# A row-gradient kernel: two transfer queues with gated loads become one queue that takes three loads and three stores in turn

## The chip, the cores and the metric

The kernel runs on one core of a Trainium2 chip. The core has a vector engine (DVE in the profile), a scalar engine (ACT), a GpSimd engine (POOL), a sync engine (SP) that computes nothing and only issues transfers, and a matrix engine that this kernel leaves idle. Sixteen DMA engines move data between the device's memory (HBM) and the on-chip buffer (SBUF, 128 partitions). An engine that issues a transfer puts it on its own queue: the profile names SP's queue q1 and ACT's queue q10. The metric is the time of one execution on the device, in microseconds; lower is better.

## The reference

```python
def setup_inputs():
    return {
        "x": np.random.randn(8192, 8192).astype(np.float32),
    }

def reference(x: np.ndarray) -> np.ndarray:
    return np.gradient(x, axis=1)
```

Along each row of 8192 numbers, an inner result is half the difference of its right and left neighbour, `(x[j+1] - x[j-1]) / 2`. The first result is `x[1] - x[0]` and the last is `x[8191] - x[8190]`, without the half. The input has 268.44 MB and so has the output; nothing is reused between rows.

## The kernel before

A tile is 256 rows: each of the 128 partitions holds `R = 2` consecutive rows, 16384 floats or 64 KB in one contiguous run, 8.39 MB in all. There are `nsets = 32` tiles and `NB = 3` buffers, the slots; tile i lives in slot i % 3. A slot is 64 floats longer than a tile: the input lies at offset `SH = 64` and the result is written over it at offset 0, so one slot serves for the load, the arithmetic and the store of its tile.

Each tile goes through five steps.

- `load` (line 69) brings the tile in. It is issued by SP, on q1.
- `put_aside` (line 78), on POOL, computes the four end differences of each partition (two rows, left and right) from the input and keeps them in `ends`. It waits for the load.
- `halve` (line 90), on DVE, is one custom instruction that subtracts and halves over the whole tile, 16382 numbers in each partition. It waits for `put_aside`, because it overwrites the input.
- `place` (line 104) copies the four kept ends over the wrong values that `halve` left at the row ends. It runs on ACT for odd tiles and on DVE for even ones.
- `store` (line 108) sends the tile out. It is issued by ACT, on q10, for the tiles 0 to 30.

The order of work is written out by hand inside a critical section with semaphores of its own (lines 44 to 54). The first three loads are issued at once. Each later load is gated by two waits of SP:

```python
                nc.sync.wait_ge(ld[(i - 1) % NB], 16 * ld_n[(i - 1) % NB])
                nc.sync.wait_ge(st[k], 16 * st_n[k])
```

The first of these (line 67) holds load i back until load i - 1 has landed, so that after the first three never more than one load is under way. The second (line 68) waits until the store of tile i - 3 has left the slot. The DMA engines thus find loads on q1 and stores on q10 and serve both queues at the same time.

The last tile is treated apart: it is halved, placed (on ACT) and stored in four pieces of half a row, 16 KB in each partition, and these four stores are issued by SP on q1. At the end SP waits for every store (lines 134 to 137).

Of the kernel before, what the change touches and what calls it, by code (L numbers as in the profile page):

```python
# [1 line left out]

# [4 lines left out]


@with_exitstack
def kernel(  # L10
    ctx: ExitStack,
    tc: tile.TileContext,
    x: bass.AP,
    out: bass.AP,
):

    nc = tc.nc
    P = nc.NUM_PARTITIONS
    n, m = x.shape
    R = 2
    NB = 3  # L30
    SH = 64
    W = R * m
    PIECES = 2 * R
    nsets = n // (P * R)
    f32 = x.dtype

    x_sets = x.rearrange("(s p t) m -> s p (t m)", p=P, t=R)
    out_sets = out.rearrange("(s p t) m -> s p (t m)", p=P, t=R)

    pool = ctx.enter_context(tc.tile_pool(name="pool", bufs=1))  # L40
    slots = [pool.tile([P, SH + W], f32, name=f"slot{k}", tag=f"slot{k}") for k in range(NB)]
    ends = pool.tile([P, nsets, R, 2], f32, name="ends", tag="ends")

    with tc.tile_critical():  # L44
        ld = [nc.alloc_semaphore(f"ld{k}") for k in range(NB)]
        st = [nc.alloc_semaphore(f"st{k}") for k in range(NB)]
        st_last = [nc.alloc_semaphore(f"st_last{q}") for q in range(PIECES)]

        aside = [nc.alloc_semaphore("aside"), 0]
        halved = [nc.alloc_semaphore("halved"), 0]  # L50
        placed = {
            nc.vector: [nc.alloc_semaphore("placed_dve"), 0],
            nc.scalar: [nc.alloc_semaphore("placed_act"), 0],
        }

        def done(ins, counter):
            ins.then_inc(counter[0])
            counter[1] += 1
            return counter[0], counter[1]

        ld_n, st_n = [0] * NB, [0] * NB

        def load(i):
            k = i % NB
            if i >= NB:

                nc.sync.wait_ge(ld[(i - 1) % NB], 16 * ld_n[(i - 1) % NB])
                nc.sync.wait_ge(st[k], 16 * st_n[k])  # L68
            nc.sync.dma_start(out=slots[k][:, SH : SH + W], in_=x_sets[i]).then_inc(ld[k], 16)
            ld_n[k] += 1  # L70

        def put_aside(i):

            k = i % NB
            xin = slots[k][:, SH : SH + W].rearrange("p (t m) -> p t m", m=m)
            nc.gpsimd.wait_ge(ld[k], 16 * ld_n[k])
            return done(
                nc.gpsimd.tensor_sub(  # L78
                    out=ends[:, i, :, :],
                    in0=xin[:, :, 1 : m : m - 2],  # L80
                    in1=xin[:, :, 0 : m - 1 : m - 2],
                ),
                aside,
            )

        def halve(b, c0, c1, ready):

            nc.vector.wait_ge(*ready)
            return done(
                nc.vector._custom_dve(  # L90
                    dve_ops.TENSOR_TENSOR_REDUCE_SUB_MAX,
                    out=b[:, c0:c1],
                    in0=b[:, SH + c0 + 1 : SH + c1 + 1],
                    in1=b[:, SH + c0 - 1 : SH + c1 - 1],
                    s0=0.0,
                    s1=0.5,
                ),
                halved,
            )

        def place(engine, out, in_, ready):
            engine.wait_ge(*ready)
            copy = nc.scalar.copy if engine is nc.scalar else nc.vector.tensor_copy
            return done(copy(out=out, in_=in_), placed[engine])  # L104

        def store(engine, i, c0, c1, ready, sem):
            engine.wait_ge(*ready)
            engine.dma_start(out=out_sets[i, :, c0:c1], in_=slots[i % NB][:, c0:c1]).then_inc(sem, 16)

        for i in range(NB):  # L110
            load(i)
        for i in range(nsets):
            k = i % NB
            b = slots[k]
            at = put_aside(i)
            if i < nsets - 1:
                at = halve(b, 1, W - 1, at)
                rows = b[:, 0:W].rearrange("p (t m) -> p t m", m=m)
                at = place(nc.scalar if i % 2 else nc.vector, rows[:, :, 0 : m : m - 1], ends[:, i, :, :], at)
                store(nc.scalar, i, 0, W, at, st[k])  # L120
                st_n[k] += 1
            else:

                step = W // PIECES
                for q in range(PIECES):
                    c0, c1 = q * step, (q + 1) * step
                    row, right = divmod(q, 2)
                    at = halve(b, c0 + 1 - right, c1 - right, at)
                    edge = c1 - 1 if right else c0
                    put = place(nc.scalar, b[:, edge : edge + 1], ends[:, i, row, right : right + 1], at)  # L130
                    store(nc.sync, i, c0, c1, put, st_last[q])
            if i + NB < nsets:
                load(i + NB)
        for k in range(NB):
            nc.sync.wait_ge(st[k], 16 * st_n[k])
        for q in range(PIECES):
            nc.sync.wait_ge(st_last[q], 16)


# [1 line left out]
_INS = ['x']  # L141
_OUTS = [((8192, 8192), 'float32')]


# [23 lines left out]
```

## Time and profile before

| what | value |
|---|---|
| median of four executions | 1251.9 us (1250.61 to 1252.5) |
| the profiled execution | 1250.61 us |
| its span in the profile | 1248.5 us |
| moved | 268.44 MB read, 268.44 MB written, mean 430 GB/s |
| DVE busy | 554.4 us, 44% of the span |
| `halve` of a whole tile, x31 | 17224 ns each |
| `halve` of a quarter tile, x4 | 4424 ns each |
| `put_aside`, x32 | 199 ns each |
| `place` on ACT (four ends), x15 / on DVE, x16 | 198 ns / 172 ns each |
| transfers: loads / stores of a tile / stores of a quarter | 32 / 31 / 4 |

The profile lists the instructions of one execution with their times. The span runs from the first to the last thing the core did; about 2 us of the execution's time lie around it. Besides instructions the trace has a record of each packet that a DMA engine moved: its queue, start, duration and size. A tile transfer consists of 128 packets of 64 KB, eight on each of the 16 DMA engines, and one record of 4 bytes per DMA engine that counts up the semaphore. The engine's name is not in a packet's record, but on each DMA engine the next packet starts 4 ns before the recorded end of the one before, so the records can be strung into 16 sequences.

### The profile page before, as it was taken

How to read it: one execution, taken by the hardware profiler on the slowest of the kernel's cores; microseconds unless marked ns; L12 is line 12 of the kernel's file. 1: busy time of each engine (PE TensorE's matmuls, PEld its weight loads, DVE VectorE, ACT ScalarE, POOL GpSimd, SP SyncE). 2: the span in 40 equal slices, each digit the busy share in tenths (PEclk: the TensorE clock that was granted, in tenths of full speed). 3: DMA queues.
4: the chain of work that ended last, by engine and by line, in shares of the span. 5: the costliest groups of instructions: out<-in, count | busy, mean ns of one | idle time of the engine just before them, and what ended most of it. 6: DMA issues, size and time to landing. Idle time of an engine off the chain costs nothing.

```text
span 1248.5 us, 259 instructions
## 1 busy us (share of the span) xinstructions
DVE 554.4 (44%) x51; ACT 5.0 (0%) x20; POOL 6.6 (1%) x36
## 2 busy tenths in 40 slices
DVE  2841452445533455334553345543355433554235
ACT  0000000000000000000000000000000000000000
POOL 0000000000000000000000000000000000000000
DMA  9999999999999999999999999999999999999998
GB/s 403 437 437 437 426 435 420 428 430 437 437 435 435 428 435 424 428 435 437 433 428 430 435 433 428 437 437 435 437 426 430 437 435 422 437 420 437 437 437 370
DMA packets 9649, 536.88 MB, mean 430 GB/s; under 512 B 1072, under 2 KB 1072, under 8 KB 1072
## 3 DMA queue, kind: packets, MB, share of 16 engines
q1 hardware_dynamic: 5184, 276.83, 51.7%
q10 hardware_dynamic: 4464, 260.05, 48.1%
q14 instruction: 1, 0.01, 0.0%
HBM read 268.44 MB, written 268.44 MB: 430 GB/s over the span
## 4 chain that ended last, share of the span: by engine, by line
DMA 96%; DVE 3%; issue 0%; POOL 0%; ACT 0%; SPq 0%
DMA slot<-in_x_dram 93%; DMA out_dram<-slot 3%; DVE slot L90 3%; POOL ends L78 0%; ACT slot L104 0%; DVE slot L104 0%; SPq L163 0%; SPq L68 0%; SPq L44 0%
## 5 line engine op out<-in xcount | busy, mean ns | idle before, releaser
L90 DVE CUSTOM_DVE_ANT_0 slot<-slot 128x16382 f32<-128x16382 f32 (+1 forms) x35 | 551.6, 15761 | 680.7 <-POOL ends L78 680.6
L78 POOL TENSOR_TENSOR ends<-slot 128x4 f32<-128x4 f32 x32 | 6.4, 199 | 1211.0 <-DMA slot<-in_x_dram 1211.0
L104 ACT COPY slot<-ends 128x4 f32<-128x4 f32 (+1 forms) x19 | 3.7, 196 | 1189.8 <-DVE slot L90 1189.8
L104 DVE COPY slot<-ends 128x4 f32<-128x4 f32 x16 | 2.7, 172 | 0.5
L104 ACT ACT_TABLE_LOAD x1 | 1.3, 1283 | 41.1 <-DVE slot L104 41.1
L152 POOL MEMSET const-uint8-127<- 128x1 uint8 x1 | 0.1, 102 | 0.0
L152 POOL MEMSET const-bfloat16-1.0<- 128x1 bf16 x1 | 0.1, 101 | 0.0
L152 POOL MEMSET const-float32-0.0<- 128x1 f32 x1 | 0.1, 98 | 0.2 <-issue 0.2
L152 POOL MEMSET const-float32-1.0<- 128x1 f32 x1 | 0.1, 98 | 0.0
## 6 DMA issues: line engine op xcount, KB each, us to landing
out_dram<-slot SPq DMA_DIRECT2D x4, 2048.0 KB, 10.2
slot<-in_x_dram SPq DMA_DIRECT2D x32, 38.8
out_dram<-slot ACTq DMA_DIRECT2D x31, 38.0
```

Source lines behind the costliest of these rows:

```text
L78: nc.gpsimd.tensor_sub(out=ends[:, i, :, :], in0=xin[:, :, 1 : m : m - 2], in1=xin[:, :, 0 : m - 1 : m - 2],),
L90: nc.vector._custom_dve(dve_ops.TENSOR_TENSOR_REDUCE_SUB_MAX, out=b[:, c0:c1], in0=b[:, SH + c0 + 1 : SH + c1 + 1], in1=b[:, SH + c0 - 1 : ...
L104: return done(copy(out=out, in_=in_), placed[engine])
L152: nc = _bacc.Bacc("TRN2", target_bir_lowering=False, num_devices=1)
```

## The change

All transfers are issued by SP and stand in one queue. In steady state SP issues three stores, then three loads, then three stores, and so on; the loads of tiles 3, 4 and 5 stand behind the stores of tiles 0, 1 and 2. A load waits for the store that frees its slot and no longer for the load before it. ACT does nothing any more: `place` runs on POOL for tiles with i % 5 equal to 1 or 3 among the first 30, and for tile 30, and otherwise on DVE. The last two tiles, not one, are halved, placed and stored in pieces, and a piece is now a whole row of each partition (32 KB) instead of half a row: 34 stores instead of 35. The semaphores are no longer set by hand; a framework derives them from the order of the code and from the dependences named in `chain`.

```diff
-        def load(i):
-            k = i % NB
-            if i >= NB:
-
-                nc.sync.wait_ge(ld[(i - 1) % NB], 16 * ld_n[(i - 1) % NB])
-                nc.sync.wait_ge(st[k], 16 * st_n[k])
-            nc.sync.dma_start(out=slots[k][:, SH : SH + W], in_=x_sets[i]).then_inc(ld[k], 16)
...
-        def store(engine, i, c0, c1, ready, sem):
-            engine.wait_ge(*ready)
-            engine.dma_start(out=out_sets[i, :, c0:c1], in_=slots[i % NB][:, c0:c1]).then_inc(sem, 16)
...
+    def chain(i, ins, *needed):
+        group, engine = f"slot{i % NB}", ins.ins.engine
+        keep = [o.ins for o in needed]
+        if in_front.get(engine, (None,))[0] == group:
+            keep.append(in_front[engine][1])
+        tc.declare_no_dep(ins.ins, group=group, keep=keep, reason="implied by the needed step")
+        tc.add_to_no_dep_group(group, ins.ins)
+        in_front[engine] = group, ins.ins
+        return ins
+
+    def load(i):
+        b = slots[i % NB]
+        ins = nc.sync.dma_start(out=b[:, SH : SH + W], in_=x_sets[i])
+        loads.append(chain(i, ins, *([stores[i - NB]] if i >= NB else [])))
...
+            at = [chain(i, ins, loads[i])]
+            last = i >= nsets - 2
+            nr = 1 if last else R
+            for r in range(0, R, nr):
+                c0, c1 = r * m + 1, (r + nr) * m - 1
...
+                halved = chain(i, ins, *at)
+                res = b[:, r * m : (r + nr) * m].rearrange("p (t m) -> p t m", m=m)
+                placer = nc.gpsimd if i % 5 in (1, 3) and not last or i == nsets - 2 else nc.vector
+                ins = placer.tensor_copy(out=res[:, :, 0 : m : m - 1], in_=ends[:, i, r : r + nr, :])
+                placed = chain(i, ins, halved)
+                ins = nc.sync.dma_start(
+                    out=out_sets[i, :, r * m : (r + nr) * m], in_=b[:, r * m : (r + nr) * m]
+                )
+                stores[i] = chain(i, ins, placed)
+                at = [halved]
+            if i % NB == NB - 1:
+                for k in range(i + 1, min(i + 1 + NB, nsets)):
+                    load(k)
```

More of the change, by code (lines that the diff above doesn't have):

```diff
@@ L4 @@
 import concourse.tile as tile
-from concourse import bass_utils, dve_ops, mybir
+from concourse import bass_utils, dve_ops
 from concourse._compat import with_exitstack
@@ L32 @@
     W = R * m
-    PIECES = 2 * R
     nsets = n // (P * R)
@@ L42 @@
     ends = pool.tile([P, nsets, R, 2], f32, name="ends", tag="ends")
[L44 to L61, printed above, removed]
-        def load(i):
-            k = i % NB
-            if i >= NB:
-                nc.sync.wait_ge(ld[(i - 1) % NB], 16 * ld_n[(i - 1) % NB])
[L68 to L83, printed above, removed]
-            )
[L86 to L90, printed above, removed]
@@ new lines @@
+    loads, stores = [], [None] * nsets
+    in_front = {}
+    def chain(i, ins, *needed):
[11 more added lines that the diff above has]
+        loads.append(chain(i, ins, *([stores[i - NB]] if i >= NB else [])))
@@ new lines @@
+    with tc.manual_schedule():
+        for i in range(NB):
+            load(i)
+        for i in range(nsets):
+            b = slots[i % NB]
+            xin = b[:, SH : SH + W].rearrange("p (t m) -> p t m", m=m)
+            ins = nc.gpsimd.tensor_sub(
+                out=ends[:, i, :, :],
+                in0=xin[:, :, 1 : m : m - 2],
+                in1=xin[:, :, 0 : m - 1 : m - 2],
+            )
+            at = [chain(i, ins, loads[i])]
[3 more added lines that the diff above has]
+                c0, c1 = r * m + 1, (r + nr) * m - 1
+                ins = nc.vector._custom_dve(
@@ L96, in halve @@
                     s1=0.5,
[L97 to L101, printed above, removed]
-            engine.wait_ge(*ready)
-            copy = nc.scalar.copy if engine is nc.scalar else nc.vector.tensor_copy
-            return done(copy(out=out, in_=in_), placed[engine])
-        def store(engine, i, c0, c1, ready, sem):
-            engine.wait_ge(*ready)
-            engine.dma_start(out=out_sets[i, :, c0:c1], in_=slots[i % NB][:, c0:c1]).then_inc(sem, 16)
@@ L110 @@
[L110 to L137, printed above, removed]
+                )
[3 more added lines that the diff above has]
+                ins = placer.tensor_copy(out=res[:, :, 0 : m : m - 1], in_=ends[:, i, r : r + nr, :])
@@ L141 @@
+                placed = chain(i, ins, halved)
+                ins = nc.sync.dma_start(
+                    out=out_sets[i, :, r * m : (r + nr) * m], in_=b[:, r * m : (r + nr) * m]
+                )
+                stores[i] = chain(i, ins, placed)
[3 more added lines that the diff above has]
+                    load(k)
 _INS = ['x']
```

## The prediction

> **What bounds the kernel now.** I read the page first, for the busy shares and the DMA slices.
>
> ```profile
> DVE 554.4 (44%) x51; ACT 5.0 (0%) x20; POOL 6.6 (1%) x36
> DMA  9999999999999999999999999999999999999998
> GB/s 403 437 437 437 426 435 420 428 430 437 437 435 435 428 435 424 428 435 437 433 428 430 435 433 428 437 437 435 437 426 430 437 435 422 437 420 437 437 437 370
> ...
> q1 hardware_dynamic: 5184, 276.83, 51.7%
> q10 hardware_dynamic: 4464, 260.05, 48.1%
> ...
> DMA 96%; DVE 3%; issue 0%; POOL 0%; ACT 0%; SPq 0%
> ```
>
> The DMA engines are busy in every slice and the chain that ended last is 96% transfers; DVE works 44% of the span. So only DMA time counts. But the slices are not all alike: the best have 437 GB/s, many 420 to 430, the first and last 403 and 370. Whatever one queue can win lies in that difference.
>
> Next the windows, one with loads alone, one with both directions, one with stores alone (start:end, length, engines, clock, DMA share, GB/s):
>
> ```profile
> 23.00:42.30 19.30, 17.40 (x2) 1.17 (x1) 0.20 (x1) 1.00 1.01 435
> 597.10:1100.60 503.50, 224.94 (x19) 1.38 (x7) 2.59 (x13) 1.00 1.00 433
> 1236.00:1244.00 8.00, 0.00 (x0) 0.00 (x0) 0.00 (x0) 1.00 1.01 432
> ```
>
> Loads alone, stores alone (in 16 KB packets) and both together run at the same rate within 1%. A direction by itself is neither faster nor slower, so sorting transfers by direction wins nothing in rate.
>
> Then the chain in order of time, for the pace:
>
> ```profile
> 1023.12 38.78 DMA slot<-in_x_dram
> 1061.90 0.01 issue
> 1061.92 38.65 DMA slot<-in_x_dram
> 1100.57 0.02 issue
> 1100.59 38.81 DMA slot<-in_x_dram
> ```
>
> A load and a store together take 38.65 us at their best, 19.3 us each. SP's waits say why load follows load: it waits for the load before (576.9 us) or for the slot's store (589.2 us).
>
> ```profile
> SPq L68 <- DMA out_dram<-slot: 589.2, 29, 79.3
> SPq L69 <- DMA slot<-in_x_dram: 576.9, 28, 22.4
> ```
>
> **Where the DMA time goes**, from the packet records strung into 16 sequences. An undisturbed 64 KB packet is recorded with 2418 ns and the next starts 4 ns before its end: 2.414 us of pace. A 16 KB packet has 611 ns (0.607 of pace). A semaphore record costs 6 ns. On each DMA engine that is 63 x 8 x 2.414 + 32 x 0.607 + 67 x 0.006 = 1216.7 + 19.4 + 0.4 = 1236.5 us. The first packet starts at 1.97 us, and there is no idle gap worth counting (one of 0.4 us on one DMA engine). Durations above the undisturbed ones add up to 6.72 us per DMA engine: 1.97 + 1236.5 + 6.72 = 1245.2, and the DMA engines end between 1244.9 and 1246.3. From there to the end of the span are 2.15 us.
>
> The 6.72 us are nearly all in load packets. Sorted by neighbour on their DMA engine: the first packets of all 0.77 (each about 2418 + 770 ns, at an empty start); a load packet that a store packet follows 5.62 us, over 147 such places per engine; loads followed by loads 0.11; store packets, also those followed by a load, 0.05. Of the 5.62, 0.69 fall at 43.9 us, when q10 gets its first store and all 16 engines stretch one load packet by 490 to 920 ns. The rest stands where a transfer of one queue begins or ends beside the other: a load packet followed by the first store packet after another load has 99 ns above normal on average (30 places per engine, 2.96 us), one inside a strict load-store alternation 23 ns, and there only in some packets. So what is lost is 5.95 us beyond the start, in the meeting of two queues.
>
> **The change part by part.**
>
> *One queue, always filled.* The order is L0 L1 L2, S0 S1 S2, L3 L4 L5, and so on to S27 S28 S29, L30 L31, four half stores. Does it run dry? From a load's landing to its store's first packet: POOL 0.2 + DVE 17.22 + `place` 0.17 to 0.2 + about 1.0 from issue to first packet (0.95 to 1.97 at the start) + some 0.1 between = 18.7 us. When load 3 lands, loads 4 and 5 are in front of store 3: 38.6 us. Slack 20 us, the same for stores 4 and 5, which each have two transfers in front. A load waits for the store three places ahead; at that moment two transfers (38.6 us) are in front of it, and issue to first packet takes 1.0 us. So the queue always holds one full transfer or more. SP issues in order, 0.33 us each; the load that waits for store 3 stands behind store 5 on SP, issued 18 us after load 5 landed, and store 3 itself lands 19.3 us after: nothing is held up. The dropped gate on the previous load costs nothing to drop. POOL's copy of 4 numbers is not in the trace; its own subtraction of the same size has 0.2 us, and even 1 us would go into the 20 us slack. On POOL it stands before the next `put_aside`, whose load lands 19.3 us after the last one while the copy ends after 17.8: no wait. The removed ACT work (5.0 us) was off the chain.
>
> *What the two queues lost.* With one queue the 5.95 us go, all but what turns of direction cost. There are 11 turns from load to store per DMA engine and 10 from store to load. For load to store the rows say 99 ns at a first store, 0.92 us at worst, 0 at best; I take 0.1: 11 x 0.1 = 1.1 us (0 to 10). For store to load the nearest rows are 2 ns (load packets behind store packets in both queues) and, at an engine with nothing before it, 0.77: I take 0, since both transfers are long in the ring; 0 to 7.7.
>
> A boundary between transfers inside one queue has rows already: at 22 us (load 0 to load 1) and at 1235 and 1240 us (quarter stores, with nothing left on q10) the 4-byte record takes 9 ns and the next packet starts 6 ns after it.
>
> Here the Trainium skill has a rule against this change. "DMA: Bandwidth & Descriptors", in the section on queues, rings and completion order, says that the semaphore's increment is a strongly ordered write that lands only after every earlier write of that DMA engine, and its section on the anatomy of a DMA puts most of about 2 us down to this receipt, worst with HBM. If that held up the ring itself, 33 store ends with no second queue to cover them would cost an estimated 66 us on top of the sum, some 1313 us. The 6 ns at the quarter stores say that the next packet does not wait for it, and the sum goes by them.
>
> *The tail.* Work per DMA engine: 62 x 8 packets x 2.414 = 1197.3, plus 4 x 8 packets of 32 KB at 1.21 (between 0.607 and 2.414 by size) = 38.7, plus 66 x 0.006 = 0.4: 1236.4, 0.1 less than before. A row of `halve` is 8.7 us (from 17224 ns for 16382 and 4424 for 4095 numbers). Tile 30's rows are ready 10.1 and 18.9 us after its load, when load 31 (19.3 us) and then also row one's store (9.7 us) are still in front; tile 31's rows the same behind tile 30's 19.3 us. Slack 9 us or more. Before, the last tile's first quarter was ready at 1222.6 while q10 still had bytes of store 30: no gap there either, so the new tail wins nothing.
>
> *The start and the end.* SP's first load needs one no-op and one branch less: 0.15 us at most. The 2.15 us after the last packet stay; bounds -0.5 and +1.
>
> **Sum.** -5.95 (stretched packets) + 1.1 (11 turns) - 0.1 (packets) = -4.95 us. Span 1248.5 - 4.95 = 1243.5; the profiled execution 1250.61 - 4.95 = 1245.7. That execution was the fastest of four and 1.3 us under the median, so for the median I say 1251.9 - 4.95 = 1247.0 us, 0.4% less. What a measurement can tell from no change is 0.2%, 2.5 us.
>
> **Rivals.**
>
> *The stretch stays.* The excess belongs to reading and writing HBM in one stretch of time or to each start of a transfer, not to two queues. For: it varies from 0 to 0.27 us per 20 us stretch without a fixed pattern. Against: the load-only start (20 to 40 us) has 0.04, and load-to-load boundaries 0. Or the turns cost 0.2 to 0.4 us each: 21 x 0.28 = 5.9 eats the gain. Time: 1249.4 to 1254.4, about 1252.
>
> *Slower: every turn is a fresh start.* If the read side cannot run ahead across a turn inside one queue, each of 21 turns pays what an empty engine paid at 2 us, 0.77: 16.2 us, 1251.9 - 5.95 + 16.2 = 1262. It makes the kernel slower by 0.2% from 0.40 us a turn. For: at 43.9 us one turn cost 0.69 on every DMA engine. Against: 1865 load packets behind and before stores have 23 ns on average, store to load 2.
>
> *The queue runs dry.* If stores took over 38 us from landing to first packet, each group of three would idle. Nothing on the way is longer than 17.22 us; at 20 us late it would begin to cost, and 10 us in each of 10 groups would be 1347. I give it next to nothing.
>
> **How the numbers follow.** Forecast 0.66, its own range 1244.5 (all 5.95 gone, turns free, less 1.4 us that medians scatter) to 1249.4; no measurable change 0.15; slower 0.19, of which fresh starts 0.15, the rest a dry queue or a slower stretch of 58 us of stores (the trace shows 18 us of them). The range for 8 in 10 takes the forecast and the middle case: 1244.5 to 1254.
>
> **What will show it.** Right: the chain's load steps become 19.3 us inside a group and 77.2 us from the last load of one group to the first of the next; every slice but the first and last has 435 to 437 GB/s; the stretch per DMA engine falls from 6.7 to about 2 us, the span to 1243.5. Wrong: load or store packets at a turn with 300 ns or more above normal (fresh starts), gaps in the records at a turn (dry), or store packets above 2418 ns in the middle of a store group.

## The result, and the profile after

The changed kernel takes 1248.24 us (median of 52 executions, 1246.73 to 1249.68); the kernel before takes 1250.25 us over the 78 executions beside it. The ratio is 0.998 with an interval of 0.9976 to 0.9985: 0.2% faster, 2.0 us. I had said 0.4%, 4.95 us. The sign and the range held; the size is 40% of what I had said, and the way there is not the one I described.

The page of the changed kernel (span 1247.1 us, its execution 1249.3 us, one of its slower ones):

```profile
span 1247.1 us, 244 instructions
...
DMA  9999999999999999999999999999999999999989
GB/s 404 437 435 433 427 420 437 437 437 435 429 431 433 425 435 437 435 435 431 433 435 433 433 429 433 437 437 435 427 437 437 429 427 435 437 433 431 437 387 404
...
q1 hardware_dynamic: 9504, 536.88, 99.7%
```

One queue carries everything. The slices are a little evener than before, but those of 420 to 430 are still there, and there is a new dip before the end (387). The chain in order of time shows the pace I had foretold. With one queue it can't name most of its releasers and calls them "another core or an unknown queue"; that is a transfer here:

```profile
645.73 77.00 another core or an unknown queue
722.73 0.07 issue
722.80 0.21 POOL ends L70
...
859.09 19.08 another core or an unknown queue
878.18 0.07 issue
878.24 0.21 POOL ends L70
```

Inside a group a load lands 19.3 us after the one before it, and from the last load of a group to the first of the next it takes 77.2 us. So the queue does not run dry, and SP's waits (372.5 us for stores to free a slot, 470.9 + 356.2 = 827 us for results) cost nothing in the middle of the run.

```profile
SPq L94 <- DVE slot L92: 470.9, 20, 38.5
SPq L60 <- DMA out_dram<-slot: 372.5, 29, 19.0
SPq L94 <- POOL slot L92: 356.2, 13, 56.2
```

The packet records say where the time went. Means are over the 16 DMA engines:

| us per DMA engine | before | predicted | after |
|---|---|---|---|
| first packet starts | 1.97 | 1.8 to 2.0 | 1.73 |
| packets at undisturbed pace | 1236.5 | 1236.4 | 1236.4 |
| stretch of packets, mean | 6.72 | 1.9 | 4.64 |
| of it at turns from load to store | 5.6 (every meeting of the queues) | 1.1 | 3.4 |
| idle, mean | 0 | 0 | 2.79 |
| last packet ends, first to last engine | 1244.9 to 1246.3 | | 1245.7 to 1245.9 |
| from there to the end of the span | 2.15 | 2.15 | 1.28 |

Two lines were not in my sum: 2.79 us of idle, and 0.87 us less after the last packet. And the mean is the wrong line to add up. The 16 engines now differ: their stretch runs from 3.3 to 6.9 us, and the one with 6.9 us, 5.9 of them at turns, idles only 0.1 us and sets the end.

The idle lies before the stores of tile 30. The timeline of the changed kernel there (start, duration, engine, line):

```profile
1188.41 17.41 DVE L81 CUSTOM_DVE_ANT_0 slot<-slot 128x8190 f32<-128x8190 f32 x2 [59.84 <-POOL ends L70]
1197.16 8.91 POOL L92 COPY slot<-ends 128x2 f32<-128x2 f32 x2 [8.79 <-DVE slot L81]
1205.89 19.89 SPq L94 DMA_DIRECT2D out_dram<-slot  x4
```

The chain has POOL's first copy by itself:

```profile
1188.41 8.70 DVE slot L81
1197.11 0.05 issue
1197.16 8.70 POOL slot L92
```

POOL's first copy of two numbers starts 0.03 us after DVE's second row and lasts 8.70 us, until 0.04 us after that row has ended. So row 0 of tile 30 is stored 17.7 us after its load has landed, not 10.1. Engines that had finished load 31 from 1202.8 us on wait up to 4.0 us; the last one finishes at 1207.1, when the store is there, and does not wait.

### The profile page after: what moved, and what is told of

Read it like the earlier page. It is cut to its first block, busy times and chain, and to the rows that moved or that the text cites. A ratio compares the mean times of both kernels' runs of the same rounds, so it can differ in the third digit from the quotient of the medians.

```text
span 1247.1 us, 244 instructions
## 1 busy us (share of the span) xinstructions
DVE 554.8 (44%) x54; POOL 17.7 (1%) x50
## 4 chain that ended last, share of the span: by engine, by line
another core or an unknown queue 74%; DVE 19%; DMA 3%; POOL 1%; issue 0%; SPq 0%; POOLq 0%
DVE slot L81 19%; DMA slot<-in_x_dram 3%; POOL slot L92 1%; POOL ends L70 0%; SPq L60 0%; DVE slot L92 0%; POOLq L127 0%
## 5 line engine op out<-in xcount | busy, mean ns | idle before, releaser
L92 POOL COPY slot<-ends 128x4 f32<-128x4 f32 (+1 forms) x14 | 11.2, 798 | 216.7 <-DVE slot L81 216.6
L92 DVE COPY slot<-ends 128x4 f32<-128x4 f32 (+1 forms) x20 | 3.4, 171 | 0.7
```

The source lines that it names most:

```text
L92: ins = placer.tensor_copy(out=res[:, :, 0 : m : m - 1], in_=ends[:, i, r : r + nr, :])
```

## The experiments

**1. Is the idle before the last stores worth anything?** Two runs take POOL away from beside DVE: DVE itself places tile 30, or ACT does.

```diff
-                placer = nc.gpsimd if i % 5 in (1, 3) and not last or i == nsets - 2 else nc.vector
+                placer = nc.gpsimd if i % 5 in (1, 3) and not last else nc.vector
```

> The changed kernel with one edit: place of tile 30 runs on DVE instead of POOL, so that it no longer stands beside a halve. Theory A (the DMA engine that ends last sets the time): in the changed kernel 15 of 16 DMA engines idle up to 4.0 us before tile 30's stores (2.8 us on average), but the last one idles 0.1 us, so the idle goes and the time stays: 1248.2 us within 0.6, and the DMA engines then end up to 4 us apart. Rival B (the mean DMA engine counts, as my prediction summed): 2.8 us less, about 1245.4 us.

Measured: 1248.25 us (1247.58 to 1249.14), ratio 0.9978 (0.9968 to 0.9989). The timeline of this run:

```profile
1187.01 8.69 DVE L81 CUSTOM_DVE_ANT_0 slot<-slot 128x8190 f32<-128x8190 f32 x1 [59.81 <-POOL ends L70]
1195.73 0.17 DVE L92 COPY slot<-ends 128x2 f32<-128x2 f32 x1
1195.81 8.68 DVE L81 CUSTOM_DVE_ANT_0 slot<-slot 128x8190 f32<-128x8190 f32 x1
1195.93 28.47 SPq L94 DMA_DIRECT2D out_dram<-slot  x4
```

The first store goes out 9.2 us after the load's landing instead of 17.7, no engine idles there any more, and the time is what it was, to 0.01 us in the medians. The engines now end between 1241.2 and 1244.5 us. (This execution, 1247.58 us, is the fastest of its twelve, and the profiled one of the changed kernel one of its slowest, so the ends of the two are not compared.) 2.8 us of idle per engine were worth nothing, because the latest engine had none: theory A. For this kernel, bound by 16 engines that work independently, the mean of their time is not its time.

```diff
-                ins = placer.tensor_copy(out=res[:, :, 0 : m : m - 1], in_=ends[:, i, r : r + nr, :])
+                copy = nc.scalar.copy if i == nsets - 2 else placer.tensor_copy
+                ins = copy(out=res[:, :, 0 : m : m - 1], in_=ends[:, i, r : r + nr, :])
```

> The changed kernel with place of tile 30 on ACT, beside DVE's halve of the next row. Theory P (a POOL instruction that moves SBUF data cannot run beside this DVE instruction, which is why POOL's copy took 8.70 us; ACT can): the first copy takes about 0.2 us, the first row's store of tile 30 is issued about 9.2 us after load 30 has landed instead of 17.7, no idle before tile 30's stores, and the time is that of tail_dve, 1248.2 us within 1. Rival (any engine that reads ends or writes into the tile waits for DVE there): 17.7 us again.

One execution, 1247.97 us. The timeline of this run:

```profile
1186.75 17.41 DVE L81 CUSTOM_DVE_ANT_0 slot<-slot 128x8190 f32<-128x8190 f32 x2 [59.85 <-POOL ends L70]
1195.47 0.20 ACT L93 COPY slot<-ends 128x2 f32<-128x2 f32 x1 [1193.45 <-DVE slot L81]
1195.69 28.82 SPq L95 DMA_DIRECT2D out_dram<-slot  x4
```

The same copy in the same place takes 0.20 us on ACT, and on POOL 8.71 us again in `turns_16` and `turns_30` below. So it is POOL that cannot work beside this DVE instruction. The Trainium skill has this in "SBUF — State Buffer", section "Who interferes with whom": a DVE instruction with two SBUF inputs contends with a GpSimd instruction that reads SBUF, and the port pair that the two share is an exclusive lock. The trace agrees: `halve` reads two inputs and the copy reads `ends`; 8.70 us is one row of `halve`. The trace of before never had POOL at work beside DVE.

**2. What is the framework worth by itself?** The same order of transfers with semaphores by hand in a critical section, as the kernel before has them.

```diff
             if i >= NB:
-                nc.sync.wait_ge(ld[(i - 1) % NB], 16 * ld_n[(i - 1) % NB])
                 nc.sync.wait_ge(st[k], 16 * st_n[k])
...
+                store(nc.sync, i, r * m, (r + nr) * m, put, st_last[2 * (i % 2) + r] if last else st[k])
...
+            if i % NB == NB - 1:
+                for j in range(i + 1, min(i + 1 + NB, nsets)):
+                    load(j)
```

> The order of the changed kernel (one queue, three loads and three stores in turn, last two tiles in rows, tile 30 placed on DVE as in the run tail_dve), but with semaphores by hand in a critical section as the kernel before has it. Theory A (leaving the critical section is worth about 1.05 us of the change's 2.0: SP's first transfer at 0.74 instead of 0.95 us, and 0.88 instead of 1.80 us from SP's last wait to the end of the span): 1249.3 us, span about 1 us longer than that of tail_dve for the same end of the transfers. Rival B (all of the gain is the queue's): 1248.25 us as tail_dve.

Measured: 1249.22 us (1248.73 to 1250.28), ratio 0.999 (0.9981 to 0.9999). The two runs stood on different chips and their intervals overlap, but the medians are 0.97 us apart where 1.05 was expected, and the trace says where it is: 2.2 us from the last packet to the end of the span in this run, 1.3 in `tail_dve`, and a first packet at 1.97 us instead of 1.74. So by the medians about half of the change's 2.0 us comes from leaving the semaphores by hand and their critical section (the run does not separate these two) and only about half from the queue.

**3. Has a turn a fixed price?** The same queue with 16 and with 30 turns from load to store instead of 11.

```diff
-            if i % NB == NB - 1:
-                for k in range(i + 1, min(i + 1 + NB, nsets)):
+            if i % 2:
+                for k in range(i + 2, min(i + 4, nsets)):
                     load(k)
```

> The changed kernel with groups of two: S0 S1 L3 L4 S2 S3 L5 L6 and so on, 16 turns from load to store instead of 11, all else as it was. Theory A (each turn from load to store costs about what the changed kernel's record shows, 0.31 us on the mean DMA engine and 0.53 us on the one that ends last): 5 turns more are 1.6 to 2.7 us, so 1249.8 to 1250.9 us. Rival B (the stretch belongs to the first store of all and to long groups of loads, not to each turn): no change, 1248.2 us within 0.6.

Measured: 1249.87 us (1248.63 to 1250.5), ratio 0.9995 (0.9986 to 1.0004). By its time alone this run fits theory A and not rival B.

```diff
-            if i % NB == NB - 1:
-                for k in range(i + 1, min(i + 1 + NB, nsets)):
-                    load(k)
+            if 1 <= i < nsets - 2:
+                load(i + 2)
```

> The changed kernel with single transfers in alternation: S0 S1 L3 S2 L4 S3 L5 and so on, 30 turns from load to store instead of 11. Theory A (a fixed price for each turn): 19 turns more at 0.31 to 0.53 us are 5.9 to 10 us, so 1254 to 1258 us, and the stretch of load packets ahead of stores grows from 3.4 to 9 us or more per DMA engine. Rival B (no price for a turn as such): 1248.2 us within 0.6.

Measured: 1250.22 us (1248.5 to 1251.71), ratio 0.9995 (0.9986 to 1.0005). Theory A falls here: 19 more turns cost about 2 us, not 6 to 10, and the stretch at turns is the same in all three kernels, 3.4, 3.4 and 3.2 us per DMA engine. Rival B's 1248.2 us was not met either. The records show where the price is paid. Mean stretch at the turns of `turns_30` in order, in us, with the time by which the engines stand apart (from the first engine's last load packet to the last engine's):

```
turn        1     2     3     4     5     6     7     8     9    10    11   12 to 30
stretch  1.10  0.33  0.27  0.25  0.33  0.05  0.10  0.14  0.10  0.15  0.34   0 to 0.04
apart    0.80  0.82  1.21  1.59  2.58  3.41  3.55  3.75  3.95  4.25  4.81   4.5
```

The price is paid over the first eleven turns, a third of it at the first; after that 19 turns cost next to nothing, with the engines 4.5 us apart. That made theory D: the turn is dear when the engines make it in the same moment. The table alone does not show it: the price falls from 1.10 to 0.33 us between the first and the second turn, at the same distance. Why the medians of these two kernels are 1.6 and 2.0 us above that of `tail_dve` stays open. The profiled executions, among the fastest of their twelve, do not show it in the mean stretch; in them the last engine ends 0.9 and 1.2 us later than in `tail_dve`.

**4. Engines kept in step.** `by_hand`, with the first load of a group waiting for all three stores before it.

```diff
-                nc.sync.wait_ge(st[k], 16 * st_n[k])
+                for j in range(NB) if i % NB == 0 else (k,):
+                    nc.sync.wait_ge(st[j], 16 * st_n[j])
```

> by_hand, but the first load of each group of three waits for all three stores before it, so that the 16 DMA engines start every group of loads together, within about 1 us. The time will be some 30 us longer (10 drains of about 3 us); what counts is the stretch of the last load packet ahead of the first store at each of the 11 turns. Theory D (engines that turn to stores in the same moment hold each other up, and once they have drifted apart the price is gone): about 1.1 us per DMA engine at every turn, as at the first turn of the changed kernel, 12 us in all. Rival F (only the first store of an execution is dear): 1.1 at the first turn and 0.3 or less at the others.

One execution, 1285.29 us, 36 us longer than `by_hand` where some 30 were foreseen. The turns cost 1.15, 1.32, 1.30, 1.23, 1.07, 1.25, 1.11, 0.86, 1.20, 1.12 and 1.13 us per DMA engine, 12.7 in all, with the engines never more than 0.9 us apart. Windows of 30 us around the first, second, third and tenth turn (start:end, length, engines, clock, DMA share, GB/s):

```profile
45.00:75.00 30.00, 26.49 (x2) 0.39 (x2) 1.00 1.01 419
165.00:195.00 30.00, 26.53 (x3) 0.20 (x1) 1.00 1.01 419
285.00:315.00 30.00, 26.70 (x3) 0.20 (x1) 1.00 1.01 419
...
1125.00:1155.00 30.00, 26.68 (x2) 0.39 (x2) 1.00 1.00 419
```

419 GB/s at each of them, 1.1 us below 435. Rival F (only the first store is dear) is out.

But `in_step` differs from `by_hand` in two things: the engines stay together, and each group of loads starts on engines that have run empty (its first packet is stretched by 0.60 to 0.71 us). The second turn of `by_hand` tells which of the two is not enough. The engines stood 0.67 us apart there, as in `in_step`, but had not run empty, and it cost 0.05 us:

```profile
165.00:195.00 30.00, 28.04 (x3) 0.20 (x1) 1.00 1.01 439
```

So being close in time does not by itself make a turn dear, and theory D is not shown as it stands. What the records do show: the turns that cost 0.86 to 1.34 us, which are the eleven of `in_step` and the first one of the changed kernel, `tail_dve`, `tail_act`, `by_hand`, `turns_16` and `turns_30`, all follow a group of loads that the 16 engines began together with nothing before it. No other turn of these kernels cost more than 0.51 us.

**5. Which change of kind is dear?** Groups of loads, stores and copies inside SBUF, in one queue; this loop stands in place of the whole computation.

```diff
+        for kind in "LSCLCS" * 12:
+            for g in range(G):
+                if kind == "L":
+                    nc.sync.dma_start(out=into[g][:, :], in_=x_q[n_in])
+                    n_in += 1
+                elif kind == "S":
+                    nc.sync.dma_start(out=out_q[n_out], in_=kept[g][:, :])
+                    n_out += 1
+                else:
+                    nc.sync.dma_start(out=copied[g][:, :], in_=kept[g][:, :])
```

> No gradient is computed and only part of the output is written: one queue moves groups of four transfers of 16 KB per partition, in the sequence loads (L, HBM to SBUF), stores (S, SBUF to HBM), copies (C, SBUF to SBUF), L, C, S, twelve times. It shows at which change of kind the last packet of a group is stretched. Theory H (the stretch belongs to leaving reads of HBM): L to S and L to C are stretched, C to S is not. Rival W (it belongs to the start of writes to HBM): L to S and C to S are stretched, L to C is not. In both S to L, C to L and S to C stay below 0.05 us on average; L to S has 0.1 to 1.1 us in the early turns.

Stretch of the packets nearest to each change of kind, mean per DMA engine over 12 changes each (11 for S to L): L to S 0.25 us (0.99 at the first), L to C 0.23; C to L 0.04, C to S 0.035, S to L 0.02, S to C 0.00. Theory H: the price belongs to leaving reads of HBM, whatever is written next. Starting to write HBM (C to S) has next to none. With 16 KB packets it is spread over the last load packets. Two limits: the only turn of the dear kind in this run is the first L to S, so whether L to C has that kind too is not shown. And the second and third L to S cost 0.06 and 0.08 us with the engines 0.5 and 0.7 us apart, less than all later ones (0.10 to 0.31 us), which again speaks against theory D.

**6. Engines set apart from the start.** `tail_dve` with 14 small loads of 15, 14, ... 2 partitions in the first group.

```diff
         for i in range(NB):
             load(i)
+            for j in spread[i]:
+                nc.sync.dma_start(out=extra[at : at + j, :], in_=x[0:j, 0:1664])
+                at += j
```

> tail_dve (1248.25 us) with 14 small extra loads in the first group, of 15, 14, ... 2 partitions with 6.7 KB each, which nobody reads; if a transfer of j partitions uses j of the 16 DMA engines, they set the engines apart by some 0.25 us each, 3.5 us in all, before the first turn. Theory D (a turn is dear when the engines make it together): the first turn falls from 1.1 us to 0.3 or less and the stretch at turns from 2.8 to under 1 us per DMA engine. The engine with the most extra work sets the end: about 1.9 + 0.7 + 1236.4 + 3.5 + 0.5 = 1243.0 us, against 1244.5 in tail_dve, so 1246.5 to 1247.5 us. Rival (the spread does not matter, the price just falls with time): the turns cost as before and the extra work comes on top, 1250 to 1251.5 us.

Measured: 1251.51 us (1250.93 to 1252.47), ratio 1.0015 (1.0007 to 1.0024).

> As apart_25 with extra loads of 3.2 KB, so that the DMA engines stand 0.12 us apart, 1.7 us in all. Theory D: the first turn costs 0.2 to 0.6 us, since in the runs so far turns with a spread of 1.3 to 2.5 us cost 0.1 to 0.5; the time is 1246.0 to 1247.5 us, if the last engine's stretch falls from 5 us to 2. Rival: 1249 to 1250 us.

Measured: 1249.32 us (1248.47 to 1249.75), ratio 0.9998 (0.9989 to 1.0007).

The first turn fell as theory D has it, from 1.11 us in `tail_dve` to 0.02 in both, with the engines 3.1 and 1.5 us apart, and the stretch at all turns from 2.9 to 0.8 us with the larger loads and 1.9 with the smaller ones. This does not settle theory D: the small loads also stand between the loads of the first group, and with the smaller ones the second turn cost 0.40 us although the engines were 1.6 us apart. The windows do not settle it either. The first two lines are from `apart_25`, whose second turn has the full rate; the third is from `tail_dve`, where the same window reads no less (at a DMA share of 1.04) without any small loads:

```profile
45.00:75.00 30.00, 22.79 (x2) 0.59 (x3) 1.00 0.99 399
165.00:195.00 30.00, 26.70 (x3) 0.40 (x2) 1.00 1.00 435
...
165.00:195.00 30.00, 27.83 (x3) 0.20 (x1) 1.00 1.04 450
```

The times came out as the rival said, for a reason neither theory had. The small loads are dear: their packets of 6.7 KB took 253 to 854 ns, 548 in the middle, where I had counted 250, and load packets beside them were stretched by 3.2 us per DMA engine (the 399 in the first window); beside the smaller ones it was 0.9 us. Setting the engines apart took more than it gave.

**7. What the gate did in two queues.** The kernel before without line 67, once in the framework and once by hand.

```diff
             if i >= NB:
-                nc.sync.wait_ge(ld[(i - 1) % NB], 16 * ld_n[(i - 1) % NB])
                 nc.sync.wait_ge(st[k], 16 * st_n[k])
```

> The kernel before with two queues, its order of work and its last tile in quarters, but written as the changed kernel is (waits derived by the framework, no critical section), and without the gate that holds a load back until the load before it has landed. Theory A (the framework alone wins about 1.05 us: SP's first transfer 0.22 us earlier, and 0.8 us less from SP's last wait to the end of the span, read from the two traces): 1249.2 us against 1250.25 before, if the gate is worth nothing. Rival B (the whole gain of the change comes from the one queue): 1250.25 us.

> The kernel before without line 67, the gate that holds a load back until the load before it has landed; two queues, semaphores by hand. It tells whether the long times of ungated_framework (up to 1270 us) came with the gate's removal or with the framework. Theory G (two queues need the gate: without it two loads may stand in q1 at once and stores come to wait): 1255 to 1265 us, with single runs up to 1270. Rival (the framework's waits on reused semaphores held the two queues up): 1250.4 us as before, within 1.

Measured: 1261.33 us (1249.84 to 1270.05), ratio 1.0072 (1.0044 to 1.01) in the framework; 1252.34 us (1248.14 to 1264.39), ratio 1.0038 (1.0011 to 1.0065) by hand. Both are slower than before and scatter by 16 to 20 us, so the framework's worth could not be read here and run 2 was made for it. The profiled executions are one short and one long, and in both one engine ends well after the others. In the short one (1249.84 us) the stretch falls from 6.7 to 2.7 us per DMA engine, nearly nothing after 600 us, and ten engines end by 1240.5 us; but one ends at 1246.7. In the long one (1262.62 us) 15 engines wait 5.6 to 6.6 us until 1231 us for the last load and its first quarter of `halve`, and one engine ends at 1258.8, 8 us after the others; its packets are stretched by 20 us, those of the others by 5 to 6.5. The slices of that one:

```profile
GB/s 399 433 433 433 430 430 435 433 433 439 437 439 439 435 430 433 433 433 433 433 430 433 433 433 433 435 435 430 435 435 430 433 433 430 435 430 433 406 364 275
```

Even to the 37th slice, and then the others are out of work. The gate kept the engines together: each of its loads starts only when all 16 have landed the one before, and in the kernel before all 16 end within 1.5 us. I read the two profiles so: the gate costs stretch (the short execution without it has 4 us less) and saves the straggler. Why one engine loses 20 us stays open. The longer half of the scatter was seen in one execution only, and why the framework's version is worse than the one by hand was not looked into.

No kernel of these runs beats the changed one by more than the measurement can tell.

## Why the prediction was half right

- **What bounds it** was right, and so were the steps that said what would not happen: the queue does not run dry, a turn from store to load costs nothing (0.00 us over 10 turns), a transfer's end holds up nothing behind it. The estimate of 66 us for 33 store ends did not come true: the last packet of a store shows no stretch at all (0.00 us), and no waiting follows it (0.02 us of idle per engine in all of `tail_dve`). The 2 us that the Trainium skill gives in "DMA: Bandwidth & Descriptors", section "Anatomy of one DMA — SWDGE (gpsimd) path", are about the time until a transfer's semaphore fires, for transfers issued by GpSimd; they are no rule against this change.
- **"What the two queues lost": the 5.95 us go, all but 1.1.** This is the step that failed. The stretch of two queues did go (about 0.5 us is left beside the turns and the start), but the term for the turns, 11 x 0.1, was a third of what it measured: the 11 turns cost 3.4 us on the mean engine, not 1.1. Five of them cost 0.34 us or more, which the prediction had named as a sign of being wrong. I had taken 99 ns from places in the trace where the two queues met. The row that came nearest to the first turn was the one I had put with the rival: 0.69 us at 43.9 us, when all 16 engines stretched a packet at once. The first turn cost 1.12 and the others 0.00 to 0.51; why the others cost less, the runs do not settle.
- **The sum over the mean engine.** "Durations above the undisturbed ones add up to 6.72 us per DMA engine" held as a description of before, where the engines end within 1.5 us. I carried it over to a kernel without the gate, where stretch plus idle comes to 7.0 us on the engine that ends last. From before to after, the last packet ends only 0.46 us earlier in the two profiled executions, which are 1.31 us apart where the medians are 2.0. `tail_dve` shows that taking 2.8 us from the mean engine changes nothing.
- **"The 2.15 us after the last packet stay", start 0.15 at most.** The bounds (-0.5 and +1) were too tight: it is 0.87 us less at the end and 0.24 at the start. This made up for about 1 us of what the queue did not give. The forecast of 1247.0 us looks nearer to 1248.24 than its reasoning was: it started from 1251.9, the median of four executions, and the same kernel took 1250.25 in the 78 beside the changed one.
- **The tail.** "Wins nothing" was right in the time, by luck: the 9 us of slack were eaten by POOL's copy of 8.70 us and by 4 us of drift. I had bounded that copy by 1 us from a row in which DVE stood still.

Of the rivals, "every turn is a fresh start" had half of the place and a price near the dear turns, 0.77 us against 0.9 to 1.3 in `in_step`. But turns from store to load cost nothing, and in the changed kernel only the first turn from load to store cost as much; its 1262 us were far off.

## What to carry to other kernels

Where 16 DMA engines work through their own queues, read the last one and not the mean: idle or stretch that only the others have is free. Waiting until all engines have finished has two sides: in `in_step` each group of loads then started on empty engines and every turn to stores was dear, and the kernel before, without its gate, had one engine that fell behind. And before moving a small copy to POOL, look whether DVE runs an instruction with two inputs at that moment.

## What the runs showed of the hardware

- When all 16 DMA engines began a group of loads together with nothing before it, each lost 0.86 to 1.34 us at the turn to stores (17 turns in seven kernels; 0.02 in two more, with small loads put into the group). The other turns cost 0 to 0.51 us, with the engines 0.6 to 4.8 us apart; 19 of them in `turns_30`, with the engines 4.5 us apart, cost 0 to 0.04. In `kinds` the smaller price came with leaving reads of HBM (0.25 and 0.23 us), not with starting writes (0.035). What makes a turn dear is not settled by these runs.
- The engines do not pay alike: at the turns of the changed kernel the engine that ended last paid 5.9 us in all, the mean one 3.4.
- A packet of 6.7 KB between packets of 64 KB took 548 ns in the middle of 119, more than twice the 250 that its size would give, and stretched its neighbours.
- The four kernels with semaphores by hand in a critical section had 1.6 to 2.2 us from the last packet to the end of the span, the eight gradient kernels written with the framework 1.2 to 1.4.
